# A mixture-of-experts loop written as one sequence of half chunks with a fixed order on three engines

## The chip, the cores and the metric

The kernel runs on one core of a Trainium2 chip. The metric is the device time of one execution in microseconds. Before the change it took 2459.33, 2452.49 and 2456.84 us in three runs, a median of 2456.84.

## The reference

The kernel computes a decoder trunk of two layers over 1024 tokens of width 1024 in float32: a causal convolution mixer in layer 0, a gated linear recurrence (HGRN2) in layer 1, and behind each a mixture of experts (MoE), which is where the change lies. Every token is sent to two of 32 experts, and the rows of an expert are padded to blocks of 128:

```python
def expert_block(args):
    xb, e = args
    return (jax.nn.silu(xb @ w_gate[e]) * (xb @ w_up[e])) @ w_down[e]

y = lax.map(expert_block, (x_pad.reshape(n_blocks, MOE_BLOCK, D), block_expert)).reshape(n_rows, D)
y = (y.astype(jnp.float32) * gate_pad[:, None]).astype(h.dtype)
return jnp.zeros((T, D), h.dtype).at[tok_pad].add(y).reshape(B, S, D)
```

The gate and up weights are 1024 x 512 per expert and the down weights 512 x 1024.

## The kernel before

**A block.** Block i is the first 128 rows of one expert. Layer 0 computes 33 blocks (32 experts and one block of a list of overflowing rows), layer 1 computes 32, of which the last keeps its rows on the chip (`KEEPL`). POOL gathers the block's rows by an indirect DMA (`gather`, L622) into one of two tiles `xg`. TensorE turns them with eight transposes into `tp`, four at a time. ScalarE rounds each four to float32r (`xh`, L235) and VectorE subtracts that from the full value (`xl`, L236). The products with the gate and up weights go to `pg` and `pu`; ScalarE takes the silu of `pg` (`hh`, L654), VectorE multiplies it by `pu` (L655), TensorE turns `hh` with four transposes, and the same two steps make `hth` and `htl`. The product with the down weights goes to `pd`; ScalarE scales it by the gate (`y`, L677, 128x1024) and POOL scatters it to DRAM (`scatter`, L627).

**Weights.** A block's weights come as six chunks of 1 MB, two each of gate, up and down (`load_w`, L119, on SP's queue), into a ring of slots (`slots`) that are taken in turn; a load waits until the chunk that had its slot is split. `split` cuts a chunk into two halves of 128x1024: ScalarE writes `wh` (L223) and VectorE `wl` (L224), into four buffers each (`WB`). Each product in float32 is made of three in float32r: xh with wh, xh with wl, xl with wh (`mm_in`, L647 to L649; `mm_down`, L671 to L673). A half gives six matmuls 128x512. A block thus has 12 halves, 72 matmuls and 12 transposes on TensorE, 12 `wh`, 3 casts of 512, a silu and a y on ScalarE, and 12 `wl`, 3 subtractions of 512 and a multiplication on VectorE.

**The order.** The loop writes for block i: gather of block i+1, first chunk of the gate product, transposes of the hh of block i-1, second chunk, transposes of the rows of block i+1, the up product, silu and multiplication, the down product of block i-1, y and scatter of block i-1. This is the order of writing alone: a scheduler at build time places each instruction in its engine's queue by its own estimate of times. An engine executes its queue in that order and stops at an instruction whose inputs or buffers aren't ready. Around the loop, `gate_table` (the gates of all rows), `list_rest` (the list of overflowing rows), `mixer_consts` and `entry` are written between the blocks. In layer 1 the six loads of the last block go to slots of their own (`LSLOT`), and its gate and up products come after the down product of the block before. After the loops follow an optional loop over further listed blocks and the end of the layer.

Of the kernel before, what the change touches and what calls it, by code (L numbers as in the profile page):

```python
# [7 lines left out]
F32 = mybir.dt.float32  # L8
# [36 lines left out]
EARLY = 3        # row tiles of h that are read back before the first MoE ends  # L45
# [34 lines left out]
CONV_DVE = (1, 2)   # the vector engine  # L80
CONV_PE = (4, 5, 6, 7)    # products
# [3 lines left out]
def trunk(ctx, tc, x, conv_norm_w, conv_pw1_w, conv_pw1_b, conv_dw_w, conv_dw_b, conv_ln_g, conv_ln_b,  # L85
# [98 lines left out]
    def mixer_consts(t1, t2, t3, t4, lp):  # L184
        """what the recurrence needs of shapes and of its bounds; t1 and t2 hold 3 * 128, t3 and t4 224 words a row."""
# [6 lines left out]
        # softmax over the two layers, its cumulative sum less the first: the second one's share  # L192
# [23 lines left out]

    def split(pool, raw):
        """a chunk of weights, by halves, as its float32r part and what that leaves."""
        for i in range(2):
            hi = pool.tile([P, 1024], F32R, name="wh", bufs=WB)  # L220
            lo = pool.tile([P, 1024], F32R, name="wl", bufs=WB)
            r = raw[:, i * 1024:(i + 1) * 1024]
            nc.scalar.activation(hi, r, AF.Copy)  # L223
            nc.vector.tensor_tensor(lo, r, hi, op=OP.subtract)  # L224
            yield hi, lo
# [12 lines left out]
    def rsqrt_small(pool, v, n):  # L238
        """1/sqrt(v) for a few columns, on the vector engine alone: Newton steps, the scale left to the end."""
# [33 lines left out]
    def transpose_n(pp, src, c0, n=4, tag="tp"):  # L273
        """n [128,128] blocks of src from column block c0 on, transposed into one bank."""
# [5 lines left out]
    def rows_T(pp, src, hi, lo, cs, nb=KD, tag="tp"):  # L280
        """rows src [128, nb * 128] -> hi/lo [128, nb, cs] with columns on partitions."""
# [5 lines left out]
    def rows_mm(ps, sh, sl, w2, ks, i0=0, i1=None):  # L287
        """ps (two halves of D) = rows @ weights over contraction tiles ks, given split."""
# [19 lines left out]
    def tail_b(pool, pp, router, l, j, res, r):  # L308
        """logits of a tile from its rows: the gain of the norm lies in the weights, its scale comes last."""
# [20 lines left out]
    def route(pool, router, i0, i1, ps):  # L330
        """the experts of the rows of tiles i0 to i1 - 1, their places among the experts' rows and what goes to these."""
# [8 lines left out]
        def first_max(v, w, mx, oh):  # L340
            """oh: one-hot of the first of the largest of v [P, n, w]; mx its value."""
# [25 lines left out]
        # rank: rows before it with the same expert, in these tiles and in the tiles done  # L367
# [9 lines left out]
        # the row of y that a place goes to less 8192, in two parts  # L377
# [20 lines left out]
        if i1 == NT:  # L398
# [3 lines left out]
            # empty places: 8192 + p, out of bounds  # L402
# [3 lines left out]
        else:  # L406
            # counts of up to 8 in each row
# [37 lines left out]
    def moe_blocks(l):  # L445
        """blocks in the order in which they are computed; NE is the first one of the list."""
# [3 lines left out]

    def moe_chunks(l):
        """(expert, part) in the order in which they are used."""
        seq, prev = [], None
        blocks = moe_blocks(l)
        for e in blocks:
            gu = [(e, part, c) for part in 'gu' for c in range(2)]
            d = [(prev, 'd', c) for c in range(2) if prev is not None]
            seq += d + gu if KEEPL[l] and e == blocks[-1] else gu + d
            prev = e
        return seq + [(prev, 'd', 0), (prev, 'd', 1)]  # L460
# [12 lines left out]
    def first_chunks(l, pools, i0=0):  # L473
        """the first chunks of an MoE, as many as the pools hold."""
# [3 lines left out]
    def moe(l, router, raws, slots, after, last=None):  # L478
        """all experts of a layer; slots are the pools of its weight chunks, in turn; after is called before the end.
        Where the last block's rows stay on chip, last is called with them in two parts."""  # L480
        with ExitStack() as held:
# [26 lines left out]
            def rows_of(tbv, n, yi, ti, pool):  # L508
                """(y row + 1) in two parts -> indices; empty places get one out of bounds."""
# [9 lines left out]
            with tc.issue_after(listed):  # L519
                for key in list(order)[:1]:  # L520
                    early[key] = list(split(mp, early[key]))

# [6 lines left out]
            def gate_table(before):  # L529
                # gates: group probability times the softmax over the two  # L530
# [38 lines left out]
            def list_rest():  # L569
                # list of the blocks past an expert's first 128 rows  # L570
# [18 lines left out]
                # inclusive count == partition + 1 at an active pair  # L589
# [8 lines left out]
                # base of (expert, block) as expert*1024 + block*128 = code * 128; past the list none matches  # L598
# [6 lines left out]
                # what an entry's rows need: y row + 1 in two parts, gate in three  # L605
# [5 lines left out]
                # place of each (token, slot) over all experts: expert*1024 + rank  # L611
# [22 lines left out]
            def x_T(xg):  # L634
                xh = mp.tile([P, KD, P], F32R, name="xh")
                xl = mp.tile([P, KD, P], F32R, name="xl")
                rows_T(pp, xg, xh, xl, slice(0, P))
                return xh, xl

            def mm_in(ps, xt, raw, c):  # L640
                xh, xl = xt
                for i, (wh, wl) in enumerate(raw if isinstance(raw, list) else split(mp, raw)):
                    wh = wh.rearrange("p (k f) -> p k f", k=2)
                    wl = wl.rearrange("p (k f) -> p k f", k=2)
                    for k in range(2):
# [94 lines left out]
            for i, e in enumerate(blocks[:nb - (KEEPL[l])] + [None]):  # L740
# [10 lines left out]
                if i:  # L751
                    ht = h_T2(hs.pop(i - 1))
# [822 lines left out]
```

## Time and profile before

| | |
|---|---|
| three runs, us | 2459.33, 2452.49, 2456.84 |
| span of the profiled execution, us | 2454.5 |
| mean granted TensorE clock | 0.960 |
| busy, share of the span: PE, DVE, ACT, POOL | 91%, 76%, 60%, 21% |
| first gate product of layer 0's MoE, last silu of it, us from the start | 478.2, 1098.8 |
| first and last silu of layer 1's MoE | 1808.5, 2403.2 |
| HBM read and written | 519.66 MB, 60.42 MB |

The time of the profiled execution itself is known by its span, from the first to the last of its instructions; the three runs without a profile lie 2.0 us below it to 4.8 above. PE is TensorE's matmul, PEld its weight load, DVE VectorE, ACT ScalarE, POOL GpSimd, SP the engine that issues the loads. The two MoE loops are about half of the span; between them lies the recurrence of layer 1, from some 1100 to 1800 us, which the change leaves as it is. A share of busy time is an average over all stages, so the stages are read by themselves.

### The profile page before, as it was taken

How to read it: one execution, taken by the hardware profiler on the slowest of the kernel's cores; microseconds unless marked ns; L12 is line 12 of the kernel's file. 1: busy time of each engine (PE TensorE's matmuls, PEld its weight loads, DVE VectorE, ACT ScalarE, POOL GpSimd, SP SyncE). 2: the span in 40 equal slices, each digit the busy share in tenths (PEclk: the TensorE clock that was granted, in tenths of full speed). 3: DMA queues.
4: the chain of work that ended last, by engine and by line, in shares of the span. 5: the costliest groups of instructions: out<-in, count | busy, mean ns of one | idle time of the engine just before them, and what ended most of it. 6: DMA issues, size and time to landing. Idle time of an engine off the chain costs nothing. (4 is left out here: it accounts for less than half of the span.)

```text
span 2454.5 us, 31862 instructions
## 1 busy us (share of the span) xinstructions
PE 2237.0 (91%) x11755; PEld 1845.3 (75%) x11755; DVE 1861.1 (76%) x2525; ACT 1461.1 (60%) x2034; POOL 518.3 (21%) x331
## 2 busy tenths in 40 slices
PE   7998889699999989994799999989979999999997
PEld 6777767588887767773799999977758877777774
DVE  5999656599988778885377666673489988888887
ACT  5553145488887777784334334332358877777774
POOL 1998511311110111101100000020041111111103
PEclk9998989899999999996899999989989999999999
DMA  5111133699999999977402020106269999999985
GB/s 171 59 61 58 56 138 133 219 329 372 366 378 347 345 334 345 359 248 195 152 21 68 28 78 27 61 31 221 94 224 366 380 359 353 354 358 355 350 295 237
DMA packets 252857, 547.66 MB, mean 223 GB/s; under 512 B 27313, under 2 KB 60281, under 8 KB 252696
## 3 DMA queue, kind: packets, MB, share of 16 engines
q1 hardware_dynamic: 231412, 504.22, 58.7%
q0 software_dynamic: 18720, 33.60, 3.7%
q10 hardware_dynamic: 2564, 7.75, 0.9%
q8 instruction: 94, 1.54, 0.3%
q14 instruction: 67, 0.55, 0.1%
HBM read 519.66 MB, written 60.42 MB: 236 GB/s over the span
## 5 line engine op out<-in xcount | busy, mean ns | idle before, releaser
L224 DVE TENSOR_TENSOR wl<-wraw,wh 128x1024 fp32r<-128x1024 f32 x780 | 921.3, 1224 | 121.7 <-ACT wh L223 116.0
L223 ACT ACTIVATE wh<-wraw 128x1024 fp32r<-128x1024 f32 x780 | 795.8, 1059 | 126.3 <-PE pg L649 55.7
L647 PE MATMUL pg<-wh,xh 128*128 128x512 f32 x520 | 212.9, 409 | 17.6 <-ACT xh L235 16.8
L648 PE MATMUL pg<-wl,xh 128*128 128x512 f32 x520 | 213.3, 410 | 16.4 <-DVE wl L224 16.4
L649 PE MATMUL pg<-wh,xl 128*128 128x512 f32 x520 | 209.7, 403 | 5.6 <-DVE xl L236 5.6
L648 PE MATMUL pu<-wl,xh 128*128 128x512 f32 x520 | 206.5, 397 | 2.9 <-DVE wl L224 2.8
L672 PE MATMUL pd<-wl,hth 128*128 128x512 f32 x520 | 207.1, 398 | 2.1 <-DVE wl L224 1.7
L671 PE MATMUL pd<-wh,hth 128*128 128x512 f32 x520 | 206.4, 397 | 2.6 <-ACT wh L223 1.7
L647 PE MATMUL pu<-wh,xh 128*128 128x512 f32 x520 | 204.1, 393 | 0.0
L673 PE MATMUL pd<-wh,htl 128*128 128x512 f32 x520 | 204.1, 393 | 0.0
L649 PE MATMUL pu<-wh,xl 128*128 128x512 f32 x520 | 203.3, 391 | 0.0
L622 POOL DMA_INDIRECT xg<-xD,tidx x64 | 91.5, 1429 | 523.0 <-PE tp L277 470.8
L980 POOL TENSOR_TENSOR wraw<-wraw,tap 128x1024 f32<-128x1024 f32 x60 | 173.7, 2895 | 36.0 <-ACT tap L979 31.6
L627 POOL DMA_INDIRECT yD<-y,yidx x64 | 66.1, 1033 | 543.7 <-ACT y L677 538.1
L1247 PE MATMUL pa<-wih,xh 128*128 128x256 f32 x512 | 147.3, 288 | 2.6 <-ACT q L1228 2.6
L235 ACT ACTIVATE xh<-tp 128x512 fp32r<-128x512 f32 x146 | 84.4, 595 | 108.3 <-PE tp L277 107.6
L1247 PE MATMUL pa<-wil,xh 128*128 128x256 f32 x512 | 147.3, 288 | 0.0
L1247 PE MATMUL pa<-wih,xl 128*128 128x256 f32 x512 | 147.3, 288 | 0.0
L648 PEld LDWEIGHTS pg<-wl,xh 128*128 128x128 f32 x520 | 100.4, 193 | 48.7 <-DVE wl L224 29.6
L647 PEld LDWEIGHTS pg<-wh,xh 128*128 128x128 f32 x520 | 100.5, 193 | 41.6 <-ACT xh L235 19.4
L649 PEld LDWEIGHTS pg<-wh,xl 128*128 128x128 f32 x520 | 100.4, 193 | 30.7 <-DVE xl L236 11.1
L236 DVE TENSOR_TENSOR xl<-tp,xh 128x512 fp32r<-128x512 f32 x146 | 98.0, 685 | 31.1 <-ACT xh L235 29.7
(457 smaller groups left out, 4859.5 us busy)
## 6 DMA issues: line engine op xcount, KB each, us to landing
wraw<-in_moe_w_gate_dram SPq DMA_DIRECT2D x130, 1024.0 KB, 7.7
wraw<-in_moe_w_up_dram SPq DMA_DIRECT2D x130, 1024.0 KB, 7.9
wraw<-in_moe_w_down_dram SPq DMA_DIRECT2D x130, 1024.0 KB, 7.9
wraw<-in_hgrn_w_in_dram SPq DMA_DIRECT2D x16, 1024.0 KB, 8.1
wraw<-in_conv_pw_w_dram SPq DMA_DIRECT2D x12, 1024.0 KB, 9.8
xD<-xn SPq DMA_DIRECT2D x16, 512.0 KB, 2.9
my<-yD SPq DMA_DIRECT2D x16, 512.0 KB, 12.3
wraw<-yD SPq DMA_DIRECT2D x16, 512.0 KB, 9.8
```

The lines of the kernel that those rows point to most:

```text
L223: nc.scalar.activation(hi, r, AF.Copy)
L224: nc.vector.tensor_tensor(lo, r, hi, op=OP.subtract)
L236: turned[2] = nc.vector.tensor_tensor(lo, ps, hi, op=OP.subtract)
L622: return nc.gpsimd.indirect_dma_start(out=xg, out_offset=None, in_=xD[l][:, :], in_offset=bass.IndirectOffsetOnAxis(ap=idx, axis=0), bound ...
L647: nc.tensor.matmul(ps, xh[:, kk], wh[:, k], start=(kk == 0), stop=False)
L648: nc.tensor.matmul(ps, xh[:, kk], wl[:, k], start=False, stop=False)
L649: done = nc.tensor.matmul(ps, xl[:, kk], wh[:, k], start=False, stop=(kk == KD - 1))
L671: nc.tensor.matmul(pd[:, ns], hh[:, kk], wh[:, ns], start=(kk == 0), stop=False)
L672: nc.tensor.matmul(pd[:, ns], hh[:, kk], wl[:, ns], start=False, stop=False)
L673: turned[0] = nc.tensor.matmul(pd[:, ns], hl[:, kk], wh[:, ns], start=False, stop=(kk == KF - 1))
L980: nc.gpsimd.tensor_tensor(res[c], res[c], t, op=OP.add)
L1247: nc.tensor.matmul(pa[:, :256], x_[:, k, js], w_[:, k].rearrange("p z c -> p (z c)"), start=(k == 0 and w_ is wh and x_ is xh), stop=(k == ...
```

## The change

The loop over blocks becomes one loop over half chunks. `moe_halves` lists them in order of use; `mm_half` and `mm_down_half` are the six matmuls of one, `split_half` its `wh` and `wl`. The splits are written three halves ahead of the products (`LEAD`), into the same four buffers. `InOrder` ties each instruction of the loop on TensorE, VectorE and ScalarE to the one written before it on the same engine, without a semaphore: the scheduler keeps the written order. Loads, gathers, scatters and the operations of `gate_table`, `list_rest`, `mixer_consts` and `entry` aren't tied.

```diff
+LEAD = 3
...
+    class InOrder:
...
+            for i in self.at.bb.instructions[self.n:]:
+                if i.engine in (ET.PE, ET.DVE, ET.Activation):
+                    if i.engine in self.last:
+                        tc.add_manual_dep(i, self.last[i.engine], mybir.DependencyInfo(
+                            mybir.DependencyClass.NoSync, mybir.DependencyReason.DATA), reason="in order")
+                    self.last[i.engine] = i.name
...
+    def moe_halves(l):
...
+        for i in range(n):
+            d = part(i - 1, ('d', 0), ('d', 1)) if i else []
+            if KEEPL[l] and i == n - 1:
+                seq += part(i, ('g', 0)) + d + part(i, ('g', 1), ('u', 0), ('u', 1))
+            else:
+                seq += part(i, ('g', 0), ('g', 1), ('u', 0), ('u', 1)) + d
+        return seq if KEEPL[l] else seq + part(n - 1, ('d', 0), ('d', 1))
...
-            for i, e in enumerate(blocks[:nb - (KEEPL[l])] + [None]):
-                if e is not None:
-                    if 0 < i < nb - 1:
-                        gather(xgs[(i + 1) % 2], cols(blocks[i + 1])[0])
...
+            for n, (i, part, c, z) in enumerate(seq):
+                prepare(n + LEAD)
+                e = blocks[i]
+                s_ = ('g', 'u', 'd').index(part) * 4 + 2 * c + z
...
+                if s_ == 0:
+                    if i + 2 < nb:
+                        gather(xgs[i % 2], cols(blocks[i + 2])[0])
+                    if i and i - 1 in pus:
+                        gate_h(i - 1)
+                if s_ == 0 and i > 1 and i - 2 in pds:
+                    with inorder:
+                        finish(pds.pop(i - 2), cols(blocks[i - 2])[2], cols(blocks[i - 2])[1])
...
+                if s_ == (1 if KEEPL[l] and i == nb - 1 else 2) and i:
+                    turn_h(i - 1)
...
+                if s_ in (5, 6) and i + 1 < nb:
+                    with inorder:
+                        xt[i + 1] = x_T(xgs[(i + 1) % 2], xt.get(i + 1), s_ - 5)
```

Here `prepare(n)` issues the load of a half's chunk, where it begins one, and writes its split. A half of block i is numbered s_ = 0 to 3 for the gate, 4 to 7 for the up and 8 to 11 for the down product; the down product of block i-1 follows the up product of block i. So the y of block i-2 is written after the first half of block i, the hh of block i-1 is turned after its third, the silu comes after its fifth, and the rows of block i+1 are turned four by four after its sixth and seventh. In layer 1's last block its first gate chunk comes ahead of the down product of block 30.

TensorE around the start of a down product in layer 1, before (pg and pu are the gate and up products, pd the down product, tp what the transposes write; hh are the gated rows of the block under way, xg the gathered rows of the next one):

```order
L649 MATMUL pu<-wh,xl 128x512
L671 MATMUL pd<-wh,hth 128x512
L277 MATMUL tp<-ident,hh 128x128 x4
L277 MATMUL tp<-ident,xg_15499 128x128 x4
L672 MATMUL pd<-wl,hth 128x512
L673 MATMUL pd<-wh,htl 128x512
...
L673 MATMUL pd<-wh,htl 128x512
L277 MATMUL tp<-ident,xg_15499 128x128 x4
L671 MATMUL pd<-wh,hth 128x512
```

TensorE there after the change:

```order
L682 MATMUL pu<-wh,xl 128x512
L302 MATMUL tp<-ident,xg_15499 128x128 x4
L682 MATMUL pu<-wh,xh 128x512
...
L682 MATMUL pu<-wh,xl 128x512
L710 MATMUL pd<-wh,hth 128x512
L711 MATMUL pd<-wl,hth 128x512
```

Before, the rows are turned within the down product, in one piece with hh and again four halves' matmuls later; now they are turned within the up product, and the down product's matmuls follow each other without a transpose.

ScalarE in layer 1, over the end of a block and the start of the next, before (wh are the high parts of half chunks of weights wraw, hth and xh those of turned rows, y the scaled result):

```order
L223 ACTIVATE wh_17284<-wraw_17272 128x1024
L235 ACTIVATE xh_17356<-tp_17358 128x512
L223 ACTIVATE wh_17305<-wraw_17303 128x1024
L223 ACTIVATE wh_17315<-wraw_17303 128x1024
L235 ACTIVATE hth_17325<-tp_17327 128x512
L677 ACTIVATE y_17294<-pd_17249,gates_15497 128x1024
L235 ACTIVATE xh_17356<-tp_17365 128x512
L223 ACTIVATE wh_17336<-wraw_17334 128x1024
```

ScalarE after, from the last split ahead of a y on:

```order
L223 ACTIVATE wh_17484<-wraw_17472 128x1024
L720 ACTIVATE y_17498<-pd_17442,gates_15497 128x1024
L223 ACTIVATE wh_17505<-wraw_17503 128x1024
L223 ACTIVATE wh_17515<-wraw_17503 128x1024
L260 ACTIVATE hth_17525<-tp_17527 128x512
L223 ACTIVATE wh_17536<-wraw_17534 128x1024
L223 ACTIVATE wh_17546<-wraw_17534 128x1024
L853 ACTIVATE hh_17557<-pg_17488 128x512
L223 ACTIVATE wh_17561<-wraw_17559 128x1024
L260 ACTIVATE xh_17571<-tp_17573 128x512
L223 ACTIVATE wh_17580<-wraw_17559 128x1024
L260 ACTIVATE xh_17571<-tp_17590 128x512
```

Before, hth, y and the second xh stand next to each other, with the splits of the next block's gate product behind them. Now y, hth, the silu hh and the two xh stand with one or two splits between any two of them.

SP's loads at the end of layer 1, before (each row is one or more chunks of 1 MB):

```order
L119 DMA wraw<-in_moe_w_down_dram 128x2x1024 x2
L119 DMA wraw<-in_moe_w_gate_dram 128x4x512 x2
L119 DMA wraw<-in_moe_w_up_dram 128x4x512 x2
L119 DMA wraw<-in_moe_w_down_dram 128x2x1024 x4
L119 DMA wraw<-in_moe_w_gate_dram 128x4x512 x2
L119 DMA wraw<-in_moe_w_up_dram 128x4x512 x2
L119 DMA wraw<-in_moe_w_down_dram 128x2x1024 x2
```

SP after:

```order
L120 DMA wraw<-in_moe_w_gate_dram 128x4x512 x2
L120 DMA wraw<-in_moe_w_up_dram 128x4x512 x2
L120 DMA wraw<-in_moe_w_down_dram 128x2x1024 x2
L120 DMA wraw<-in_moe_w_gate_dram 128x4x512
L120 DMA wraw<-in_moe_w_down_dram 128x2x1024 x2
L120 DMA wraw<-in_moe_w_gate_dram 128x4x512
L120 DMA wraw<-in_moe_w_up_dram 128x4x512 x2
L120 DMA wraw<-in_moe_w_down_dram 128x2x1024 x2
```

Before, the two down chunks of the next to last block are issued ahead of all six chunks of the last block. Now the first gate chunk and one down chunk of the last block are issued ahead of the first of these two, and the second down chunk of the next to last block (the last row's last) is issued after all chunks of the last block, as its slot is the one that the first gate chunk leaves.

More of the change, by code (lines that the diff above doesn't have):

```diff
@@ L449, in moe_blocks, with part @@
         return list(range(NE - 1)) + [NE] * LISTED[l] + [NE - 1]
+    def moe_halves(l):
+        n, seq = len(moe_blocks(l)), []
+        def part(i, *chunks):
+            return [(i, p_, c, z) for p_, c in chunks for z in range(2)]
+        for i in range(n):
[5 more added lines that the diff above has]
+        return seq if KEEPL[l] else seq + part(n - 1, ('d', 0), ('d', 1))
     def moe_chunks(l):
-        seq, prev = [], None
         blocks = moe_blocks(l)
[L455 to L460, printed above, removed]
+        keys = [(blocks[i], p_, c) for i, p_, c, z in moe_halves(l) if z == 0]
+        e = blocks[-1]
+        return [k for k in keys if not (KEEPL[l] and k[0] == e)] + [
+            (e, p_, c) for p_ in 'gud' for c in range(2) if KEEPL[l]]
     def moe_src(l, e, part, c):
@@ L632, in scatter, with x_T, mm_half @@
                 scat.append(s)
[L634 to L637, printed above, removed]
-                return xh, xl
-            def mm_in(ps, xt, raw, c):
[L641 to L645, printed above, removed]
-                        kk = 4 * c + 2 * i + k
-                        nc.tensor.matmul(ps, xh[:, kk], wh[:, k], start=(kk == 0), stop=False)
-                        nc.tensor.matmul(ps, xh[:, kk], wl[:, k], start=False, stop=False)
-                        done = nc.tensor.matmul(ps, xl[:, kk], wh[:, k], start=False, stop=(kk == KD - 1))
+            def x_T(xg, xt=None, b=None):
+                xh, xl = xt or (mp.tile([P, KD, P], F32R, name="xh"), mp.tile([P, KD, P], F32R, name="xl"))
+                for b in (0, 1) if b is None else (b,):
+                    t = transpose_n(pp, xg, 4 * b).rearrange("p (a c) -> p a c", a=4)
+                    split_psum(xh[:, 4 * b:4 * b + 4], xl[:, 4 * b:4 * b + 4], t)
+                return xh, xl
+            def mm_half(ps, xt, w, kk):
+                xh, xl = xt
+                wh, wl = (t.rearrange("p (k f) -> p k f", k=2) for t in w)
+                for k in range(2):
+                    for x_, w_ in ((xh, wh), (xh, wl), (xl, wh)):
+                        done = nc.tensor.matmul(ps, x_[:, kk + k], w_[:, k], start=(kk + k == 0 and x_ is xh and w_ is wh),
+                                                stop=(kk + k == KD - 1 and x_ is xl))
+                return done
+            def mm_in(ps, xt, raw, c):
+                for z, w in enumerate(split(mp, raw)):
+                    done = mm_half(ps, xt, w, 4 * c + 2 * z)
                 return done
@@ L721, in cols, with prepare @@
                 return first["e"][1][:, 0:1], first["e"][2][:, 0:1], first["e"][3][:, 0:1]
-            xt, hs = {}, {}
-            gather(xgs[0], cols(0)[0])
+            xt, hs, pgs, pus, pds = {}, {}, {}, {}, {}
+            inorder = InOrder()
+            seq = moe_halves(l)
+            raw_of, ready = {}, {}
+            def prepare(n):
+                if n >= len(seq):
+                    return
+                i, part, c, z = seq[n]
+                key = (blocks[i], part, c)
+                if KEEPL[l] and i == nb - 1 and key not in order_last:
+                    for k_, at in zip([(key[0], p_, c_) for p_ in 'gud' for c_ in range(2)], LSLOT[l]):
+                        order[k_] = at
+                        order_last[k_] = early[k_] = get(k_)
+                if z == 0:
+                    raw_of[key] = get(key)
+                with inorder:
+                    ready[n] = split_half(mp, raw_of[key], z)
+            order_last = {}
+            with tc.issue_after(listed):
+                for n in range(LEAD - 1):
+                    prepare(n)
+            g0 = gather(xgs[0], cols(0)[0])
             g1 = gather(xgs[1], cols(1)[0])
-            xt[0] = x_T(xgs[0])
+            with inorder:
+                xt[0] = x_T(xgs[0])
+            prepare(LEAD - 1)
             if KEEPL[l]:
@@ new lines, in turn_h, with gate_h @@
+            def turn_h(i):
+                with inorder:
+                    hs[i] = h_T2(hs[i])
+            def gate_h(i):
+                with inorder:
+                    nc.vector.tensor_tensor(hs[i], pus.pop(i), hs[i], op=OP.mult)
+            for n, (i, part, c, z) in enumerate(seq):
+                prepare(n + LEAD)
+                e = blocks[i]
+                s_ = ('g', 'u', 'd').index(part) * 4 + 2 * c + z
+                with inorder:
+                    if part == 'g':
+                        if s_ == 0:
+                            pgs[i] = pp.tile([P, FE], F32, name="pg", bufs=PGB)
+                        done = mm_half(pgs[i], xt[i], ready.pop(n), 4 * c + 2 * z)
+                    elif part == 'u':
+                        if s_ == 4:
+                            pus[i] = pp.tile([P, FE], F32, name="pu", bufs=PGB)
+                        mm_half(pus[i], xt[i], ready.pop(n), 4 * c + 2 * z)
+                    else:
+                        if s_ == 8:
+                            pds[i] = pp.tile([P, D], F32, name="pd", bufs=3 - PGB)
+                        mm_down_half(pds[i], hs[i], ready.pop(n), 2 * c + z)
+                if s_ == 0:
+                    if i + 2 < nb:
[3 more added lines that the diff above has]
+                if s_ == 0 and i > 1 and i - 2 in pds:
+                    with inorder:
+                        finish(pds.pop(i - 2), cols(blocks[i - 2])[2], cols(blocks[i - 2])[1])
+                if i == 0 and s_ == 1:
+                    with tc.issue_after(g1.ins):
+                        gate_table(done.ins)
+                    rp.release()
+                    rp = apool(f"rest{l}", 1)
+                if s_ == (1 if KEEPL[l] and i == nb - 1 else 2) and i:
+                    turn_h(i - 1)
+                if s_ == 4:
+                    hs[i] = mp.tile([P, FE], F32, name="hlast" if KEEPL[l] and i == nb - 1 else "hh", bufs=HB)
+                    with inorder:
+                        nc.scalar.activation(hs[i], pgs.pop(i), AF.Silu)
+                if s_ in (5, 6) and i + 1 < nb:
+                    with inorder:
+                        xt[i + 1] = x_T(xgs[(i + 1) % 2], xt.get(i + 1), s_ - 5)
+                if s_ == 8 and i + 1 in pus:
+                    gate_h(i + 1)
+                    if i + 1 == nb - 1:
+                        last_turn = n + 2
+                if KEEPL[l] and s_ == 11 and i == nb - 2:
+                    with inorder:
+                        finish(pds.pop(i), cols(blocks[i])[2], cols(blocks[i])[1])
+                if not KEEPL[l] and s_ == 11 and i == nb - 2:
+                    turn_h(nb - 1)
+                if s_ == 11 or (i == 0 and s_ == 7):
+                    i += s_ == 11
@@ L778, in moe @@
                 e = blocks[-1]
-                keys = [(e, part, c) for part in 'gud' for c in range(2)]
-                for key, pool in zip(keys, LSLOT[l]):
-                    order[key] = pool
-                    early[key] = get(key)
-                pg = pp.tile([P, FE], F32, name="pg", bufs=PGB)
-                pu = pp.tile([P, FE], F32, name="pu", bufs=PGB)
-                for c in range(2):
-                    mm_in(pg, xt[nb - 1], get((e, 'g', c)), c)
-                for c in range(2):
-                    mm_in(pu, xt[nb - 1], get((e, 'u', c)), c)
-                hlast = h_T(pg, pu, "hlast")
+                gate_h(nb - 1)
+                hlast = hs[nb - 1]
+            else:
+                for i in (nb - 2, nb - 1):
+                    if i in pds:
+                        with inorder:
+                            finish(pds.pop(i), cols(blocks[i])[2], cols(blocks[i])[1])
             left = after()
```

62 lines of the change are left out of this document (25 added, 37 removed).

## The prediction

> **What bounds the kernel now.** I read the page first, then busy time by stretches, then the silu of each block (ScalarE runs one per block, so the starts of the silus are a clock of the loop), then waits and a timeline. The change touches the two MoE loops alone. Stretches (columns: length, then PE, PEld, DVE, ACT and POOL busy, granted clock, DMA share, GB/s):
>
> ```profile
> 600.00:700.00 100.00, 100.00 (x488) 82.15 (x487) 93.02 (x112) 85.19 (x96) 13.32 (x12) 1.00 1.03 370
> 800.00:900.00 100.00, 89.29 (x393) 70.81 (x392) 77.72 (x76) 71.61 (x81) 11.88 (x10) 0.95 0.95 336
> 1900.00:2000.00 100.00, 99.24 (x473) 82.15 (x473) 90.33 (x90) 83.19 (x95) 12.57 (x11) 1.00 1.02 376
> 2100.00:2200.00 100.00, 93.97 (x423) 72.94 (x423) 83.24 (x82) 75.16 (x87) 11.34 (x10) 1.00 0.99 357
> ```
>
> TensorE is the bound, and each loop has a good stretch, where it never stops, and bad ones, where it stands idle for 5 to 11 us in 100. No other engine is full in the bad ones. The silu rows price a block (count, then first and last start):
>
> ```profile
> L654 ACT ACTIVATE hh<-pg x33: 573/578/598, 489.1 to 1098.8; 128x512 f32<-128x512 f32 x33
> L654 ACT ACTIVATE hh<-pg x31: 573/598/606, 1808.5 to 2380.1; 128x512 f32<-128x512 f32 x31
> L654 ACT ACTIVATE hlast<-pg x1: 598/598/598, 2403.2 to 2403.2; 128x512 f32<-128x512 f32 x1
> L654 ACT ACTIVATE hh<-pg x5: 575/578/582, 611.8 to 684.0; 128x512 f32<-128x512 f32 x5
> L654 ACT ACTIVATE hh<-pg x7: 573/578/588, 1844.4 to 1950.7; 128x512 f32<-128x512 f32 x7
> L654 ACT ACTIVATE hh<-pg x2: 575/586/598, 489.1 to 501.4; 128x512 f32<-128x512 f32 x2
> L654 ACT ACTIVATE hh<-pg x2: 577/588/598, 1808.5 to 1826.0; 128x512 f32<-128x512 f32 x2
> ```
>
> Layer 0 takes 609.7 us for 32 intervals (33 silus). Layer 1 takes 571.6 for 30, and its last, 2380.1 to 2403.2, 23.1: 594.7. The means are 19.05 and 19.18. The good stretches give 72.2 / 4 = 18.05 and 106.3 / 6 = 17.72. The first interval of a layer is short (12.3 in layer 0), since no block before has a down product.
>
> What a block costs TensorE, and one bad boundary (start, duration, tile, idle before):
>
> ```profile
> 911.53 0.39 PE L672 MATMUL pd<-wl,hth 128*128 128x512 f32 x1
> 911.76 0.39 PE L673 MATMUL pd<-wh,htl 128*128 128x512 f32 x1
> 911.99 1.03 PE L277 MATMUL tp<-ident,xg 128*128 128x128 f32 x8
> 912.19 1.11 ACT L677 ACTIVATE y<-pd,gates 128x1024 f32<-128x1024 f32 x1 [0.30 <-PE pd L673]
> 913.20 1.05 ACT L223 ACTIVATE wh<-wraw 128x1024 fp32r<-128x1024 f32 x1
> 914.15 1.07 ACT L235 ACTIVATE xh<-tp 128x512 fp32r<-128x512 f32 x2
> 914.28 1.23 DVE L224 TENSOR_TENSOR wl<-wraw,wh 128x1024 fp32r<-128x1024 f32 x1 [1.13 <-ACT wh L223]
> 914.79 0.50 PE L647 MATMUL pg<-wh,xh 128*128 128x512 f32 x1 [1.76 <-ACT xh L235]
> 915.42 1.28 DVE L236 TENSOR_TENSOR xl<-tp,xh 128x512 fp32r<-128x512 f32 x2
> 916.16 0.50 PE L649 MATMUL pg<-wh,xl 128*128 128x512 f32 x1 [0.64 <-DVE xl L236]
> ```
>
> Matmuls of 512 start 0.227 us apart, transposes (1.03 - 0.27) / 7 = 0.108. With 72 matmuls and 12 transposes a block can't be under 16.3 + 1.3 = 17.6. At 912 the next rows are turned at the very end of a block: ScalarE has a y and a wh in front of xh, VectorE a wl in front of xl, and TensorE waits 1.76 and 0.64 us. The waits (total, times, longest), first of 600 to 1060, then of 1900 to 2380:
>
> ```profile
> SPq L119 <- DVE wl L224: 383.7, 137, 7.2
> DVE wl L224 <- ACT wh L223: 57.8, 60, 2.7
> PE pg L647 <- ACT xh L235: 15.0, 8, 2.7
> PE pg L649 <- DVE xl L236: 5.0, 9, 0.8
> ...
> DVE wl L224 <- ACT wh L223: 36.6, 60, 1.3
> PE pg L648 <- DVE wl L224: 13.1, 21, 0.8
> PE tp L277 <- DVE hh L655: 5.9, 10, 0.6
> PE pu L648 <- DVE wl L224: 2.5, 14, 0.2
> ```
>
> TensorE waits for turned rows in layer 0 and for low parts, or for the gated hh, in layer 1. It never waits for a load: SP stood 383.7 of 460 us waiting for a slot to come free.
>
> **Part by part.** *Order and lead.* No product is added or removed: a block stays 72 matmuls, 12 transposes, 12 wh, 12 wl, 3 casts and 3 subtractions of 512, silu, hh and y. What moves is when. Durations, from 1900 to 2380:
>
> ```profile
> L224 DVE TENSOR_TENSOR wl<-wraw,wh 128x1024 fp32r<-128x1024 f32 x299 | 348.7, 1219 | 37.2 <-ACT wh L223 36.6 <-DMA wraw<-in_moe_w_up_dram 0.3
> L223 ACT ACTIVATE wh<-wraw 128x1024 fp32r<-128x1024 f32 x299 | 299.2, 1058 | 13.9 <-PE pu L649 6.9 <-PE pg L649 4.5 <-DVE wl L224 1.2
> L677 ACT ACTIVATE y<-pd,gates 128x1024 f32<-128x1024 f32 x25 | 27.8, 1112 | 0.0
> L235 ACT ACTIVATE xh<-tp 128x512 fp32r<-128x512 f32 x50 | 29.9, 599 | 71.4 <-PE tp L277 71.3
> L236 DVE TENSOR_TENSOR xl<-tp,xh 128x512 fp32r<-128x512 f32 x50 | 34.4, 689 | 11.6 <-ACT xh L235 10.7
> L655 DVE TENSOR_TENSOR hh<-pu,hh 128x512 f32<-128x512 f32 x25 | 17.2, 686 | 22.7 <-PE pu L649 22.7
> ```
>
> A half is split three halves ahead with four buffers, so the wh of half n+3 waits for TensorE's half n-1. From that half's end: 0.3 us to ScalarE (the idle at 912.19), wh 1.06, wl 1.22, 2.6 us in all. TensorE needs it three halves later, 18 x 0.227 = 4.08. With one y (1.11) in front it is 3.7, and still in time; with an xh that waits for its four transposes (0.43 + 0.3 + 0.60, during which TensorE also spends 0.43) it is 3.6 of 4.5. So the wl waits of layer 1 (13.1 + 2.5) go.
>
> *Rows turned mid-block.* The eight transposes lie after the second and the third half of pu, with six and five halves (8.2 and 6.8 us) left before the next pg. xh and xl need 0.3 + 0.60 + 0.69 and, with a wh and a wl in front of each, some 4 us. So the waits of layer 0 (15.0 + 5.0, and the half clock behind them, 0.95 in 800:900) go. The wait that this adds is ScalarE's on the transposes, with one or two wh queued behind; ScalarE has 83.19 us of work in 100, so 3 us of slack a block. Turning hh after three halves of pg gives VectorE 4.08 us for one hh of 0.69 and the wl in front: the 5.9 goes too.
>
> *Gathers two blocks ahead, before the scatter on POOL.* A rows tile is free once it is turned mid-block, and its next gather is issued at the start of the block after, more than a block before the transposes that read it.
>
> ```profile
> xg<-xD,tidx POOLq DMA_INDIRECT x64, 7.4
> ```
>
> It needs 7.4 us of the 26 or so that it has, on an engine that is busy 12 us in 100; the scatter now stands behind it, where nobody but the y buffers waits. I price it at 0; if a gather were a block late, its 7.4 would show, once.
>
> *What is late next.* VectorE: 90.33 busy in a stretch where blocks take 17.72, so 16.0 us a block. It has 1.7 to spare, and waited 37.2 us for wh in 25 blocks, 1.5 a block. It just fits. So I put a steady block between 17.65 (the floor, and little else) and 18.05 (the good stretch of layer 0, where small operations of the list run), and take 17.8, nearer to 17.72, as that stretch has the later loop's work alone.
>
> *Ends.* Layer 0's first interval stays 12.3. I add 2 for the first gathers behind the list's POOL work and 3 for the list, the entry and the last hh, turned without cover (bounds 0 and 8). Layer 1's first interval was 17.5, since TensorE stood behind the gate table:
>
> ```profile
> 1814.45 0.46 PE L560 MATMUL pd<-qg,pl 128*128 128x96 bf16 x7 [1.99 <-POOL qg L553]
> 1816.00 0.22 PE L560 MATMUL pd<-qg,pl 128*128 128x96 bf16 x1 [1.09 <-POOL pl L558]
> ```
>
> and at half clock after. The table now comes a half later in the row, where qg is nearly done: 12.3 + 0.9 = 13.2 (bounds 12.3 and 17.5). Its last interval gets longer. By its 16 halves and 12 transposes it is 23.1 as before, but the last block's first gate chunk now runs ahead of the down product of the block before, so hh is turned with nothing to cover it (1.3: cast 0.60, subtraction 0.69), and the load of that down product's second chunk waits for a slot that only this first chunk frees. It lands this much after its issue:
>
> ```profile
> wraw<-in_moe_w_down_dram SPq DMA_DIRECT2D x130, 1024.0 KB, 7.9
> ```
>
> Freed 1.5 us (4.08 - 2.6) before TensorE starts the second half of that chunk, it lands 6.4 after, and is split 2.3 later (1.06 + 1.22): 8.7, against a need at 5.8 (1.36 + 0.43 + 1.3 + 2.72). That is 3 us of stall (0 to 5): 27.4.
>
> **The sum.** Layer 0: 12.3 + 31 x 17.8 + 5 = 569.1, against 609.7: -40.6. Layer 1: 13.2 + 29 x 17.8 + 27.4 = 556.8, against 594.7: -37.9. Span 2454.5 - 78.5 = 2376.0. The median of the three runs, 2456.84, is 2.3 above the span of the profiled execution, so 2378. With 17.65 and no stumbles: 559.5 and 547.3, 97.6 less, 2359. With 18.05 and the long ends (8 and 29.4): 2378 + 15 + 5 = 2398.
>
> **Rivals.** *Loads become the bound.* A block moves 376 GB/s x 17.72 us = 6.66 MB; the sum asks for 374 GB/s all along. At 357, what layer 1 got in 2100:2200, a block takes 18.66: 60 x 0.86 = 52 more, 2430. For it: the DMA share is 0.95 to 1.03 in all four stretches. Against: 370 and 376 in the two stretches where TensorE was full, and SP waits for slots, not for landings. The Trainium skill (DMA: Bandwidth & Descriptors, Specifications) puts the limit of memory for one core at about 358 GB/s; by it a block would be 18.6 and the time 2426. The 376 in the row stands above it, and the same page says that a core streaming alone goes higher.
>
> *VectorE in a fixed order becomes the bound.* 16.0 of work plus 1.5 of waiting for wh is 17.5; if the fixed order lifts the waiting to 2.4 (one late xl or hh a block, 0.7 to 0.9, that nothing can overtake), a block is 18.4: 2378 + 36 = 2414. For it: the 57.8 and 36.6 us that wl waits; against: the lead of three halves takes up just such delays.
>
> *Slower: ScalarE's inserts come out one behind the other.* ScalarE can no longer let a ready wh pass a waiting xh, hth or y. If the chain from a freed buffer to a finished wl passes 4.08 us, which it does with two inserts in it (2.6 + 1.11 + 0.60 = 4.3), every insert shows at TensorE: 1.11 + 3 x 0.60 = 2.9 a block, 20.7 us, 60 x 2.9 = 174 more: 2552. Against: at least two wh stand between any two of y, hth and silu, and ScalarE has 3 us a block free.
>
> *The change doesn't do what it says:* the pinning orders the instructions, but the stumbles come from moments that the order doesn't touch (small operations, jitter of loads), and the loop keeps the mean of its bad stretches, some 19.1 a block: 2378 + 60 x 1.3 = 2456, no change. Against: each wait in the list above has its place in the order, and moved.
>
> **Chances.** Forecast 0.62 (2359 to 2398). VectorE 0.14. Loads 0.10. Forecast and these two are faster; with a little of the no-change case (0.02 of its 0.07) that makes 0.88, and 0.05 is left for the same. Slower 0.07. The range goes to 2430, past the VectorE case and to the loads' own price, and leaves out some 0.17. What a measurement of this kernel can tell from no change is about 0.3%, 7 us: faster 0.88, same 0.05, slower 0.07.
>
> **What would show it.** Silus 17.7 to 17.9 apart over both loops, as in the good stretches; PE at 99 in every 100 us; no wait of pg for xh or xl; SP still waiting for slots; 27 us ahead of the last silu of layer 1. Wrong if wh waits for loads (then the loads), if PE waits for wl with VectorE at 95 or more (VectorE), or if PE waits for wl while ScalarE idles behind transposes (the slower case).

## The result

The changed kernel takes 2385.53 us in the median of 4 runs (2384.56 to 2386.18) against 2456.64 before: a ratio of 0.9711, 95% interval 0.9699 to 0.9722. The forecast was 2378, with a range of 2359 to 2430.

The silus after the change (count, first and last start), each layer's, the steady stretch of each, and the last of layer 1:

```profile
L853 ACT ACTIVATE hh<-pg x33: 573/588/597, 486.7 to 1054.6; 128x512 f32<-128x512 f32 x33
L853 ACT ACTIVATE hh<-pg x31: 577/587/597, 1763.6 to 2295.9; 128x512 f32<-128x512 f32 x31
L853 ACT ACTIVATE hh<-pg x23: 577/589/592, 663.8 to 1054.6; 128x512 f32<-128x512 f32 x23
L853 ACT ACTIVATE hh<-pg x28: 577/588/595, 1816.3 to 2295.9; 128x512 f32<-128x512 f32 x28
L853 ACT ACTIVATE hlast<-pg x1: 586/586/586, 2333.5 to 2333.5; 128x512 f32<-128x512 f32 x1
```

Layer 0 takes 567.9 us (609.7 before, 569.1 forecast). Layer 1 takes 569.9 (594.7 before, 556.8 forecast). A steady block is 390.8 / 22 = 17.76 and 479.6 / 27 = 17.76. The span fell from 2454.5 to 2383.8, by 70.7: 41.8 of it in layer 0, 24.8 in layer 1, 2.4 ahead of layer 0's first silu (whose start differs as much among the kernels below, 485.5 to 489.2), and 1.7 between the loops and after them.

The stretches after the change (columns as before: length, PE, PEld, DVE, ACT and POOL busy, granted clock, DMA share, GB/s):

```profile
800.00:900.00 100.00, 100.00 (x477) 82.67 (x476) 93.28 (x91) 85.39 (x98) 15.15 (x12) 1.00 1.03 384
1900.00:2000.00 100.00, 100.00 (x476) 82.69 (x475) 93.24 (x91) 85.36 (x98) 15.78 (x12) 1.00 1.03 382
2100.00:2200.00 100.00, 100.00 (x475) 82.68 (x473) 94.07 (x91) 84.97 (x96) 15.15 (x11) 1.00 1.02 382
```

The stretch 800 to 900 had PE at 89.29 at a clock of 0.95 before; now these three look like the good ones did. The waits of 1900 to 2200 (total, times, longest):

```profile
POOL xg L656 <- PE tp L302: 125.0, 16, 7.8
POOL yD L661 <- ACT y L720: 122.6, 17, 7.3
DVE wl L224 <- ACT wh L223: 16.7, 34, 0.7
ACT xh L260 <- PE tp L302: 15.8, 34, 0.6
ACT wh L223 <- PE pd L712: 14.4, 51, 0.3
```

No wait of TensorE is left in the list. ScalarE and VectorE wait for TensorE and for each other, in short pieces, and none waits for a load there. The longest of SP's waits of 600 to 1050:

```profile
SPq L120 <- DVE wl L224: 298.4, 119, 10.6
```

With the view's rows for other operations of VectorE, SP's loads of weights wait 360 of 450 us for slots, where it was 399 of 460 before. What the loops did not give is at the end of layer 1, 37.6 us from the last but one silu to the last (2333.5 - 2295.9). The timeline there:

```profile
2306.80 0.37 SPq L120 DMA_DIRECT2D wraw<-in_moe_w_down_dram  x1
2306.80 1.07 ACT L223 ACTIVATE wh<-wraw 128x1024 fp32r<-128x1024 f32 x1 [0.29 <-DVE wl L224]
2307.77 1.10 ACT L720 ACTIVATE y<-pd,gates 128x1024 f32<-128x1024 f32 x1
2309.32 0.60 PE L302 MATMUL tp<-ident,hh 128*128 128x128 f32 x4
2319.27 1.06 ACT L223 ACTIVATE wh<-wraw 128x1024 fp32r<-128x1024 f32 x1 [10.40 <-SPq L895]
2320.23 0.58 ACT L260 ACTIVATE hth<-tp 128x512 fp32r<-128x512 f32 x1
2320.86 0.80 PE L710 MATMUL pd<-wh,hth 128*128 128x512 f32 x1 [10.94 <-ACT hth L260]
```

The load of block 30's second down chunk is issued at 2306.80. ScalarE starts its split at 2319.27, 12.5 us later (the view names an entry of SP's queue, L895, as the releaser; that it waited for this load is inferred from the order, and the first experiment bears it out). The transposes of hh were done at 2309.9, but `hth` stands behind that split in ScalarE's queue, so the first down chunk, though split long before, can't run either.

### The profile page after: what moved, and what is told of

Its sections match the earlier page's. It is cut to its first block, busy times and chain, and to the rows that moved or that the text cites. A ratio compares the mean times of both kernels' runs of the same rounds, so it can differ in the third digit from the quotient of the medians.

```text
span 2383.8 us, 31779 instructions
## 1 busy us (share of the span) xinstructions
PE 2207.5 (93%) x11755; PEld 1842.7 (77%) x11755; DVE 1870.9 (78%) x2525; ACT 1461.2 (61%) x2034; POOL 548.1 (23%) x331
## 5 line engine op out<-in xcount | busy, mean ns | idle before, releaser
L223 ACT ACTIVATE wh<-wraw 128x1024 fp32r<-128x1024 f32 x780 | 805.3, 1058 | 95.7 <-PE pd L712 59.0
L682 PE MATMUL pu<-wh,xh 128*128 128x512 f32 x520 | 215.7, 415 | 0.0
L682 PE MATMUL pg<-wl,xh 128*128 128x512 f32 x520 | 205.3, 395 | 0.1
L661 POOL DMA_INDIRECT yD<-y,yidx x64 | 81.6, 1275 | 527.4 <-ACT y L720 519.9
L656 POOL DMA_INDIRECT xg<-xD,tidx x64 | 97.4, 1522 | 450.6 <-PE tp L302 412.7
L710 PEld LDWEIGHTS pd<-wh,hth 128*128 128x128 f32 x520 | 98.8, 190 | 34.8 <-ACT hth L260 12.1
L711 PEld LDWEIGHTS pd<-wl,hth 128*128 128x128 f32 x520 | 98.7, 190 | 23.8 <-DVE wl L224 3.1
L1078 ACT ACTIVATE tap<-upl,dwT 128x1024 f32<-128x1024 f32 x60 | 68.9, 1150 | 77.9 <-POOL wraw L1079 77.9
L712 PEld LDWEIGHTS pd<-wh,htl 128*128 128x128 f32 x520 | 98.7, 190 | 21.9 <-DVE htl L261 1.3
```

Source lines behind the costliest of these rows:

```text
L656: return nc.gpsimd.indirect_dma_start(out=xg, out_offset=None, in_=xD[l][:, :], in_offset=bass.IndirectOffsetOnAxis(ap=idx, axis=0), bound ...
L661: s = nc.gpsimd.indirect_dma_start(out=yD[l][:, :], out_offset=bass.IndirectOffsetOnAxis(ap=idx, axis=0), in_=y, in_offset=None, bounds_ch ...
L682: done = nc.tensor.matmul(ps, x_[:, kk + k], w_[:, k], start=(kk + k == 0 and x_ is xh and w_ is wh), stop=(kk + k == KD - 1 and x_ is xl))
L710: nc.tensor.matmul(pd[:, ns], hh[:, kk], wh[:, ns], start=(kk == 0), stop=False)
L711: nc.tensor.matmul(pd[:, ns], hh[:, kk], wl[:, ns], start=False, stop=False)
L712: turned[0] = nc.tensor.matmul(pd[:, ns], hl[:, kk], wh[:, ns], start=False, stop=(kk == KF - 1))
```

## The experiments

Each of the twelve kernels is the changed kernel with a small edit. Where no interval is given the time is that of a single run; runs of the kernel before, on the same chips, lay between 2452.52 and 2460.91.

### The end of layer 1

```diff
                 if KEEPL[l] and i == nb - 1 and key not in order_last:
+                    for c_ in range(2):
+                        early[(blocks[i - 1], 'd', c_)] = get((blocks[i - 1], 'd', c_))
```

> The loads of block 30's two down chunks are issued ahead of the last block's six, so the second no longer waits for the slot of the last block's first gate chunk. Theory (the 13 us that layer 1's end costs beyond 24.4 are this one load, with hth queued behind the split that waits for it): last interval of the silus of layer 1 from 37.5 to 24 or 25 us, TensorE's wait of 10.94 for hth down to 1 or 2, time 2372. Rival (the wait is the turning of hh itself, or the loads at the end are slow in any order): last interval 30 or more, time 2380 to 2386.

2374.5 us (4 runs, 2373.07 to 2377.01), ratio to before 0.9667 (0.9651 to 0.9683). The last silus:

```profile
L855 ACT ACTIVATE hh<-pg x31: 579/588/597, 1762.9 to 2295.4; 128x512 f32<-128x512 f32 x31
L855 ACT ACTIVATE hlast<-pg x1: 586/586/586, 2321.5 to 2321.5; 128x512 f32<-128x512 f32 x1
```

The waits at the end, 2270 to 2340:

```profile
ACT wh L223 <- DMA wraw<-in_moe_w_gate_dram: 2.6, 1, 2.6
PE pd L710 <- ACT hth L260: 1.2, 1, 1.2
```

The last interval is 26.1, and TensorE's wait for hth is 1.2 instead of 10.9, near the 1.3 that the prediction gave to turning hh uncovered. The 2.6 is a new wait: the last block's gate chunk is now loaded behind the two down chunks. So the order of these loads is worth 11.5 us of the last interval (37.6 - 26.1).

```diff
+                turn = KEEPL[l] and i == nb - 1 and part == 'g' and 2 * c + z == 1
+                if not turn:
+                    prepare(n + LEAD)
...
                     turn_h(i - 1)
+                    if turn:
+                        prepare(n + LEAD)
```

> Loads as in the changed kernel; only the split of block 30's second down chunk is written behind the turning of hh, in the one place at the end of layer 1. Theory (order on ScalarE adds to the load's wait): hth starts near 1 us after its transposes instead of 10.9, the first down chunk's 2.7 us run under the load, the last interval falls from 37.5 to 31 to 34, time 2379 to 2382. Rival (the load alone counts): nothing changes, 2385.

2381.23 us. The last interval is 2330.6 - 2296.0 = 34.6, 3 less. The waits of 2270 to 2340:

```profile
ACT wh L223 <- SPq L899: 9.0, 1, 9.0
PE pd L710 <- ACT wh L223: 8.4, 2, 6.8
PE pd L710 <- ACT hth L260: 0.7, 1, 0.7
```

TensorE waits 0.7 for hth and then for the split of the second chunk: the first now runs under the load, as the theory had it, though the interval came out just above its 31 to 34. So of the 11.5 us that the late load costs, 3 are owed to the place of hth in ScalarE's queue.

### What the gain comes from

Nothing tied, the loop as written:

```diff
-                if i.engine in (ET.PE, ET.DVE, ET.Activation):
+                if False:
```

> The loop is written as in the changed kernel, but nothing is tied: the scheduler orders the engines. Theory (the pinned order is what removes the waits): waits of pg for xh, xl or wl come back, block 18.3 to 19, time 2410 to 2460. Rival (lead, place of the turning and early gathers are enough as written): block 17.8, time 2380 to 2390.

2455.47 us (10 runs), ratio to before 0.9994 (0.9985 to 1.0004): the whole gain is gone. A stretch of 300 us, and some of TensorE's waits in it:

```profile
1900.00:2200.00 300.00, 285.76 (x1295) 226.93 (x1294) 251.92 (x246) 230.56 (x263) 39.03 (x32) 0.99 0.99 354
```

```profile
PE pg L682 <- DVE wl L224: 7.2, 12, 0.8
PE tp L302 <- DVE hh L816: 3.9, 6, 0.9
PE pg L682 <- ACT wh L223: 1.5, 1, 1.5
```

The first two are old waits, on the pairs that TensorE waited for in layer 1 before. In layer 0 its longest wait of 600 to 1060 is back as well (before, it was 15.0, 8 times):

```profile
PE pg L682 <- ACT xh L260: 16.0, 8, 2.7
```

The new writing alone gives nothing, since the scheduler puts its own order in its place: from 1900 to 2200 TensorE turns rows of the next block within the down product or right behind it in 22 of 31 places (23 of 32 in the kernel before) and never within the up product, where they were written.

Pinned (the order tied as in the changed kernel), with a shorter lead, of two halves and three buffers, and of one half and four:

```diff
-LEAD = 3
-WB = 4
+LEAD = 2
+WB = 3
```

> Splits two halves ahead with three buffers. The chain from a freed buffer to wl is 2.6 us, the lead falls from 4.08 to 2.72. Theory of the lead (and the slower rival's mechanism): y, hth, silu and xh now come out at TensorE, some 0.6 to 1 us each, block 17.77 to 21 or 22 us, time 2570 to 2650, slower than the kernel before. Rival (the fixed order counts, not the lead): block below 18.5, time under 2430.

2423.40 us. A block is 293.1 / 16 = 18.32. The silus of 1900 to 2200, the stretch, and the waits in it:

```profile
L853 ACT ACTIVATE hh<-pg x17: 584/587/593, 1904.1 to 2197.2; 128x512 f32<-128x512 f32 x17
```

```profile
1900.00:2200.00 300.00, 300.00 (x1379) 236.89 (x1378) 274.10 (x262) 247.55 (x280) 42.74 (x33) 1.00 1.02 376
```

```profile
PEld pd L711 <- DVE wl L224: 9.8, 32, 0.3
PEld pu L682 <- DVE wl L224: 5.7, 17, 0.4
```

TensorE's weight loads wait for wl three times a block, about 0.3 each. That is the lead's theory in kind, but it costs 0.55 us a block and not 3 to 4: the rival's numbers (under 18.5 and under 2430) came true. The chain of 2.6 still fits into 2.72, and most inserts (y, hth, the silu, xh) probably run in time that ScalarE would have waited for a buffer; which of them show wasn't taken apart, nor what two halves cost with four buffers.

```diff
-LEAD = 3
+LEAD = 1
```

> Pinned as in the changed kernel, four buffers, but a half is split only one half ahead in the written order: on ScalarE and VectorE the split of half n+2 now stands behind the turned rows of half n. Theory (the slower rival of the prediction, with the lead taken away: a fixed order shows each insert that waits for TensorE): xh twice and hth once a block hold the next split, 1.3 to its start, 1.06 and 1.22 for wh and wl, 3.6 in all against the 1.8 to 2.0 that TensorE gives, 1.6 us each, block 22 to 23 us, 2640 to 2710, slower than the kernel before. Rival (buffers free early make up for it, pinning alone is enough): block 18.3 or less, under 2430.

2637.33 us, just under the theory's 2640 to 2710 and 7% slower than the kernel before. Blocks are 174.4 / 8 = 21.8. The silus of 1950 to 2150, and waits of 1900 to 2200:

```profile
L853 ACT ACTIVATE hh<-pg x9: 581/589/592, 1963.9 to 2138.3; 128x512 f32<-128x512 f32 x9
```

```profile
ACT xh L260 <- PE tp L302: 36.1, 28, 2.3
ACT hth L260 <- PE tp L302: 31.2, 13, 4.1
PE pu L682 <- DVE wl L224: 19.5, 26, 0.8
PE pg L682 <- DVE wl L224: 6.9, 14, 0.8
```

ScalarE stands at xh and hth for the transposes, the split behind them is late, TensorE waits for it, and that delays the next transposes. So pinning without the lead makes the kernel slower, and the lead written without pinning gives nothing.

The two other parts of the change, undone one at a time, everything else pinned and three halves ahead:

```diff
-                if s_ in (5, 6) and i + 1 < nb:
+                if s_ in (10, 11) and i + 2 < nb:
                     with inorder:
-                        xt[i + 1] = x_T(xgs[(i + 1) % 2], xt.get(i + 1), s_ - 5)
+                        xt[i + 2] = x_T(xgs[i % 2], xt.get(i + 2), s_ - 10)
```

(The first block's next rows keep their place.)

> The next rows are turned after the third and the fourth half of the down product instead of the up product's second and third; all else as in the changed kernel, pinned. Theory (turning mid-block is worth the wait of pg for xh and xl): between the first turning and pg lie 1.8 us, xh and xl need 1.6 plus a wh and perhaps a wl in front, so pg waits 0.8 to 2 us a block, time 2435 to 2510. Rival (pinned order and lead are enough): 2385.

2386.73 us, the rival's case. The rows are turned at the end of the down product, the trace has no wait of pg for xh, and a block is still 284.3 / 16 = 17.77:

```profile
L853 ACT ACTIVATE hh<-pg x17: 584/589/594, 1906.8 to 2191.1; 128x512 f32<-128x512 f32 x17
```

```diff
-                    if i + 2 < nb:
-                        gather(xgs[i % 2], cols(blocks[i + 2])[0])
+                    if 0 < i < nb - 1:
+                        gather(xgs[(i + 1) % 2], cols(blocks[i + 1])[0])
```

> Gathers one block ahead instead of two. Theory: a gather is issued at the start of a block and its rows are turned 8.6 us later; it needs about 7.4 to land, so it just fits: 0 to 1 us a block, 2385 to 2440. Rival (the early gather is a main part of the gain): the transposes wait several us in most blocks, 2500 or more.

2386.82 us, and again 284.3 / 16 = 17.77 a block:

```profile
L853 ACT ACTIVATE hh<-pg x17: 586/589/593, 1905.5 to 2189.8; 128x512 f32<-128x512 f32 x17
```

The place of the turning thus carries none of the gain. The second edit tests nothing, as the loop ran the same. Gathers aren't tied, and the trace has them where the changed kernel has them, 32.8 us ahead of the transposes that read them (gathers and turnings are matched by counting them from the start of the layer):

```profile
1945.33 1.62 POOL L656 DMA_INDIRECT xg<-xD,tidx  x1 [7.81 <-PE tp L302]
1978.15 0.60 PE L302 MATMUL tp<-ident,xg 128*128 128x128 f32 x4
```

The kernel before settles the matter: from 1900 to 2200 its gathers were issued 27.6 to 38.3 us ahead of their transposes, and 28.8 to 46.4 in layer 0 from its seventh block on, although it was written to gather one block ahead. They weren't late there, so gathering two blocks ahead had nothing to give in these stretches.

### What is next in line

One wl a block written twice, then two:

```diff
                     ready[n] = split_half(mp, raw_of[key], z)
+                    if part + str(2 * c + z) in ('d2',):
+                        nc.vector.tensor_tensor(ready[n][1], raw_of[key][:, z * 1024:z * 1024 + 1024], ready[n][0],
+                                                op=OP.subtract)
```

> One wl a block is written twice: 1.2 us more for VectorE in each block. VectorE is busy 93.6 us in 100, 16.6 of a block's 17.77. Theory (VectorE is next in line with 1.1 us to spare): 0 to 0.3 us a block, 2385 to 2405. Rival (TensorE alone, VectorE far off): exactly 2385 here and with two.

> Two wl a block are written twice: 2.3 to 2.4 us more for VectorE, 18.9 a block. Theory (VectorE is next in line): it becomes the bound, about 1.1 us more a block, 2440 to 2470. Rival (what a trace calls busy overstates VectorE's work, pitch 1.14 a wl, 16.0 a block): 18.3 a block, 2415 to 2425; or 2385 if VectorE is far off.

2408.80 us, just above the forecast of 2385 to 2405, and 2463.52, within its own. Silus and a stretch of the kernel with one:

```profile
L856 ACT ACTIVATE hh<-pg x17: 582/589/592, 1908.7 to 2197.1; 128x512 f32<-128x512 f32 x17
```

```profile
1900.00:2000.00 100.00, 100.00 (x467) 80.63 (x466) 98.29 (x95) 84.22 (x95) 19.78 (x11) 1.00 1.03 373
```

The same of the kernel with two:

```profile
L856 ACT ACTIVATE hh<-pg x16: 585/587/594, 1907.7 to 2190.1; 128x512 f32<-128x512 f32 x16
```

```profile
1900.00:2000.00 100.00, 96.77 (x444) 76.29 (x444) 99.13 (x96) 79.83 (x90) 17.34 (x11) 1.00 1.01 359
```

With one a block is 288.4 / 16 = 18.02, with two 282.4 / 15 = 18.83, and VectorE is 99 full. With two, VectorE is the bound, so its own work is 18.83 less two subtractions of 1.22 at most, 16.4 or a little more: it is next in line with somewhat over 1 us to spare, as the theory has it. The 93.24 busy of the changed kernel, 16.6 a block, was the better measure than the 16.0 of the prediction.

One more load of 0.39 MB a block, and two, which nothing reads:

```diff
+                if z == 0 and c == 0 and part == 'u' and i < NE - 1:
+                    more = mp.tile([P, 768], F32, name="more", bufs=1)
+                    nc.sync.dma_start(more, moe_w_down[l, i][0:P, 0:768])
```

> One more load of 0.39 MB a block that nothing reads (31 blocks a layer). The changed kernel moves 384 GB/s x 17.77 us = 6.8 MB a block; this asks for 7.2, 406 GB/s. Theory (loads have room): block 17.8, 2385 to 2390. Rival (loads are at their bound at 384): 18.8 a block, 2445.

> Two such loads a block: 7.6 MB, 428 GB/s at 17.77 us. Theory (loads have room, but not much): loads become the bound somewhere above 406, so 17.8 to 18.7 a block, 2385 to 2445, with splits that wait for loads. Rival (bound at 384): 19.8 a block, 2510.

2419.34 and 2576.59 us. These totals can't be read as forecast. The loads weren't tied, and SP's queue took many of them late: of layer 0's, 5 of 31 came behind its last silu with one a block and 36 of 62 with two, and the next stage stood 10.3 and 90.0 us behind them. Within the loops either kernel ran only about one such load in 30 to 40 us, so the 406 and 428 GB/s of the forecasts were never asked for. What can be read is the part of layer 1 where some ran among the others and splits began to wait, with one load from 2100 to 2300:

```profile
2100.00:2300.00 200.00, 194.18 (x881) 153.51 (x879) 172.05 (x169) 155.40 (x178) 25.98 (x21) 0.99 1.01 376
```

```profile
ACT wh L223 <- DMA wraw<-in_moe_w_gate_dram: 28.5, 20, 3.5
ACT wh L223 <- DMA wraw<-in_moe_w_down_dram: 7.9, 10, 2.2
```

With two, from 2150 to 2300:

```profile
2150.00:2300.00 150.00, 147.63 (x679) 117.11 (x678) 130.48 (x128) 118.84 (x136) 20.28 (x16) 1.00 1.03 384
```

```profile
ACT wh L223 <- DMA wraw<-in_moe_w_gate_dram: 13.5, 12, 1.9
ACT wh L223 <- DMA wraw<-in_moe_w_down_dram: 7.2, 7, 1.6
```

Splits wait for loads there, as they do for 0.6 us in all from 600 to 1050 in the changed kernel, and the rate, 376 and 384, doesn't rise above the 382 to 384 that the changed kernel has anyway. SP's queue isn't what holds them: with one load it stands 128 of these 200 us at slots. So in these kernels loads seem to have their limit near 380 GB/s, and the changed kernel is close to it, at 384 x 17.77 = 6.8 MB a block.

The time from a load's issue to its landing points the same way. In the kernel of 2381.23 us, whose loads stand as in the changed kernel, the page of the profile gives this median for the down loads (of those whose landing the trace tells):

```profile
wraw<-in_moe_w_down_dram SPq DMA_DIRECT2D x130, 1024.0 KB, 12.1
```

In the kernel before it was 7.9. With VectorE's added subtractions, the order and the lead being the same, it is 9.7 at 18.02 us a block and 7.5 at 18.83. From 18.83 to 17.77 us a block, loads thus take some 60% longer, while the rate rises from 359 to 383 GB/s, by 7%.

The loads' order of the first experiment, with the gate table called later:

```diff
-                if i == 0 and s_ == 1:
+                if i == 0 and s_ == 6:
```

> The loads of the first experiment, and gate_table called after the seventh half of the first block instead of the second, in both layers. Theory (TensorE still stands behind qg and pl of the gate table at the start of layer 1, about 3 to 4 us beyond its 12.3): first interval of layer 1 from 16.4 to 13, time 2366 to 2369. Rival (the table's chain on POOL is late wherever it is called, or the rows behind it come later): 2372, as the loads alone.

2373.77 us (5 runs, 2368.11 to 2375.88), ratio 0.967 (0.9657 to 0.9683): as with the loads alone, and the first interval of layer 1 is 16.6, not the 13 of the theory. The table's products stand where they stood, behind `qg`, where TensorE waited 1.81 us at 1764.58 in the changed kernel:

```profile
1760.93 0.50 PE L594 MATMUL pd<-qg,pl 128*128 128x96 bf16 x8 [1.99 <-POOL qg L587]
```

They aren't tied, so the call's place didn't move them, and what the table costs layer 1's start stays untested. These two kernels are the fastest of the study.

## Why the prediction was right, and where it was not

**The bound and the steady block** were right: TensorE at 100 in the stretches shown, 17.77 a block where 17.8 was taken, and the list's and the last turning's 5 us in layer 0 came out as 567.9 - 12.4 - 31 x 17.77 = 4.6.

**The cause was half wrong.** The step "rows turned mid-block" gave the waits of layer 0 to the place of the turning. With the turning at the end of the down product the waits are gone as well, and without pinning they stay, as the scheduler moves most of the turnings back. It is the fixed order together with the lead of three halves. The block's 17.8 was read from the good stretches and not added up from the parts; that a wrong cause for layer 0 didn't hurt the number is luck. The gathers were priced at 0, and no transpose waits for one in the list above; but "two blocks ahead" was no change to the chip, as the scheduler had put them there before.

**The ends of layer 1** are the terms that were mis-sized, by 13.4 us together, which more than covers the 7.5 between forecast and result. The last interval was put at 27.4 and is 37.6. The mechanism, a load that waits for the slot of the last block's first chunk, was right; two sizes were off. The load was taken at 7.9 us, the median of its kind in the slower kernel, and its data was used 12.5 us after issue. That is no straggler: in the loop at its new pace 12 is the median of its kind. And the sum let the first down chunk run under the load, while hth stood behind the split of the second on ScalarE: the order on one engine had been looked at for the steady block only. With the load in time 11.5 us go, and with hth ahead of the split 3 of them. After the wait, a dozen matmuls also ran 0.43 us apart instead of 0.227 (granted clock 0.53 from 2320 to 2327). As an estimate, 4.6 for the load, 2.7 for the first down chunk and 2.4 for the slow matmuls make 9.7 of the 10.2. The first interval was put at 13.2 and is 16.4: TensorE waited 1.81 us for `qg` where 0.9 was taken, and for single `pl` after it.

**The rivals.** *Slower through ScalarE's inserts* is a true mechanism with the wrong threshold. It is the lead that decides: at three halves nothing shows, at two 0.55 us a block, at one 4 us a block and 2637 us, where 2552 had been worked out. *VectorE* has a little over 1 us in hand and took none of the gain. *Loads* seem to have a bound, but near 380 GB/s and not at the 357 of the slow stretch, which was the rate the loop asked for and no limit. The 358 GB/s that the Trainium skill gives for one core (DMA: Bandwidth & Descriptors, Specifications) is below the 384 of the steady stretches, and the measurement decides; the 384 agrees with what the prediction quotes of that page, that a core streaming alone goes higher. *The change doesn't do what it says* failed by the pinning: the experiment without it gave just that case's number, 2455 us where 2456 was worked out.

## What to carry to other kernels

In this loop, where engines with little slack alternate, the scheduler's order cost 70 us, and it took a fixed order and a lead that covers the longest chain to win them; a fixed order with a lead of one half was worse than the scheduler's. What is written isn't yet what runs: look in the trace for where each part of a change, and of an experiment, ended up. Then read the fixed order once more at the ends, instruction by instruction, with every load and whatever stands behind it, since nothing can overtake there any more. Take the time of a load at the pace that the new loop will have. Before going on, add a known amount to the next engine: here one more subtraction a block shows at once.

## What the runs showed of the hardware

A PE that is busy for 300.00 of 300 us can still lose time. With a lead of two halves it issued 1379 matmuls in the stretch, the changed kernel 1421, in the row below, at the same 300.00 and a clock of 1.00. In the profile a matmul lasts 0.39 us and starts 0.227 after the one before, so gaps under 0.16 us leave no idle time. At 84 matmuls and transposes a block, 18.32 and 17.77 us a block make 1376 and 1418 in 300 us, as counted. The counts, and the busy time of PEld (236.89 against 248.03), tell such stretches apart.

```profile
1900.00:2200.00 300.00, 300.00 (x1421) 248.03 (x1419) 280.86 (x271) 255.48 (x288) 45.10 (x34) 1.00 1.02 383
```
